# Other weight pieces get their low part by an adding transfer in the first feed-forward

## The chip, the cores and the metric

The kernel runs on one core of one Trainium2 chip. The metric is the time of one execution in device microseconds, as the median of repeated runs. TensorE (PE) does the matrix products, VectorE (DVE) and ScalarE (ACT) prepare their operands, SyncE (SP) issues the plain loads, and GpSimd (POOL) issues the transfers that add to what lies in on-chip memory.

## The reference

One encoder block for 256 tokens of width 2048 in float32. It has two feed-forwards, and between them a mixer and a cross-attention. The change touches the first feed-forward alone:

```python
def swiglu(h, w_up, w_down):
    gate, up = jnp.split(h @ w_up, 2, axis=-1)
    return (jax.nn.silu(gate) * up) @ w_down

x = x + 0.5 * swiglu(rms_norm(x, ffn1_norm[l]), ffn1_w_up[l], ffn1_w_down[l])
```

`w_up` has 2048 rows and 2 x 5632 columns, `w_down` 5632 rows and 2048 columns.

## The kernel before

**Groups and pieces.** The 5632 hidden columns are worked through in 11 groups of 512. A group needs 2048 rows of `w_up`, which come in eight pieces of 1 MB, the pairs 0 to 7: 256 rows each, that is two row blocks by the gate and the up columns of the group. After the pieces of a group come pieces of `w_down` for the groups before it: two behind groups 1 and 2, four behind group 3 and each later one. A piece is identified on the list of the plan as `("fast", g, p)`, `("mixed", g, p)` or `("down", ...)`.

**High and low parts.** A float32 product is made of three products of a rounded high part and the low part that is left: high by high, high by low and low by high. In the program's names `h` is the high part of a weight piece, `l` its low part, `xh` and `xl` those of the activations. So a row `acc<-h,xh` is a product with the weight's high part, and `acc<-l,xh` one with its low part. `three` (L587 to L600) issues the products: the first loop (L597) those with the high part, the second (L599) those with the low part.

**Seven or eight products.** A fast piece computes its 2 x 2 block product with seven block products (each as three products: 21), and needs for that differences of the weight's blocks: VectorE makes them in `td` (L321, L323, L325), and ScalarE and VectorE split `td` into the high part `h` (two halves, L146) and the low part `tl` (two halves, L147). A mixed piece does eight block products (24 products) with the weight as it is, with no `td`. Both add into the same seven PSUM banks of the group.

**Two ways to the low part.** In a piece without an adding transfer VectorE subtracts: `l = raw - h` (L147). In a piece with one, ScalarE writes the negative rounded weight into `l` (L330 for fast pieces, L276 for mixed ones), and POOL issues a transfer that adds the weight from memory once more (L331, L277), which leaves the low part. The low products of such a fast piece stand behind those with `tl`; for pair 6 they are held back into the next piece (`three(products, 3 if adds(...) else 0, ...)`). For a mixed piece with an adding transfer, load, negation and transfer begin one piece earlier (`begin_added`, L270).

**What sets the order.** The letters of `FIRST` (L46) list a group's pieces in their order: `f` fast, `a` fast with an adding transfer, `m` mixed, `M` mixed with an adding transfer, each followed by its pair. `first` (L50) turns them into the plan; `adds` (L77) asks for the letter `a`. `weights` (L240) prepares two pieces ahead. A scheduling layer then fixes the order of the instructions on each engine, which run strictly in that order. Buffers bound how far the preparation runs ahead: three of `h` (also used for the high part of `td`), three of `l`, three of `wide` (for `td`, `tl` and the evacuation), and four for loads (three `raw`, one `raw1`). A buffer is free again when TensorE, ScalarE or VectorE has read it for the last time.

```python
PIECES = "f1 a3 f0 a4 f2 a5 a6 f7"
...
KINDS = {"m": "mixed", "M": "mixed", "f": "fast", "a": "fast"}
...
def adds(name, e):
...
    return e[0] == "fast" and (name == "ffn1" or e[1] > 3) and f"a{e[2]}" in FIRST[e[1]]
```

The second feed-forward takes its own lists for groups 0 to 3, and `FIRST` for the later ones. The end of a group evacuates its seven banks (L679 to L691), forms the activation (L629, L630), turns it with TensorE (L637) and splits it into `hidop` (L641, L642). L707 adds a finished quarter to the residual `x`.

## Time and profile before

| | |
|---|---|
| median of 3 runs | 2431.85 us (2431.12 to 2434.92) |
| the profiled execution's own time | 2430.69 us |
| its span | 2428.9 us |
| TensorE busy | 2404.3 us, 99% |
| VectorE busy | 2025.2 us, 83% |
| ScalarE busy | 1542.3 us, 63% |
| mean granted clock of TensorE | 0.996 |

The profile lists the busy time of each engine, groups of instructions with the idle time ahead of them and what ended it, a chain of work that ended last, and tables by stretches of time. Products are pipelined: a product lasts about 0.39 us in the records, though the next one starts after some 0.23 us, so a busy TensorE need not be working at its best pace. A row of the list in order of time gives start, duration, engine, line and operands, and in brackets the idle time ahead and what ended it. In a row of the chain the numbers are start and duration.

### The profile page before, as it was taken

The numbers are of one execution on the slowest core, as the hardware profiler recorded it, in microseconds if no ns is written. First come the engines' busy times: TensorE is split into PE (matmuls) and PEld (weight loads), VectorE is DVE, ScalarE is ACT, GpSimd is POOL, SyncE is SP. The second block draws the span as 40 slices with busy tenths as digits, with TensorE's granted clock in tenths as the row PEclk, the third lists the DMA queues.
The fourth block names the chain that finished last, engine by engine and source line by source line (L and its number), as shares of the span: only waits on it lengthen the run. The fifth ranks groups of instructions, "written<-read, shape, count | busy, mean of one in ns | idle before, by whom it ended". The sixth has DMA issues, their size and how long they took to land.

```text
span 2428.9 us, 30888 instructions
## 1 busy us (share of the span) xinstructions
PE 2404.3 (99%) x12068; PEld 1997.9 (82%) x12068; DVE 2025.2 (83%) x2273; ACT 1542.3 (63%) x1564; POOL 118.7 (5%) x172
## 2 busy tenths in 40 slices
PE   9999999999999999999999999999999999999998
PEld 7887777888888888888888888888888888888887
DVE  7768898999999866768678666675799999999995
ACT  7756666777777664444476434555676677777774
POOL 0000000000000000000000000100000000000000
PEclk9999999999999999999999999999999999999999
DMA  8877778999999857666768766875588889999993
GB/s 306 309 249 238 243 214 252 276 276 276 276 276 277 280 193 275 243 258 232 262 244 290 294 245 244 301 266 190 200 323 312 308 273 280 273 275 268 273 278 136
DMA packets 98450, 636.62 MB, mean 262 GB/s; under 512 B 10944, under 2 KB 11456, under 8 KB 33536
## 3 DMA queue, kind: packets, MB, share of 16 engines
q1 hardware_dynamic: 74160, 493.61, 54.8%
q0 software_dynamic: 24000, 140.78, 23.7%
q8 instruction: 94, 1.54, 0.2%
q14 instruction: 52, 0.43, 0.1%
q10 hardware_dynamic: 144, 0.26, 0.0%
HBM read 597.77 MB, written 36.83 MB: 261 GB/s over the span
## 4 chain that ended last, share of the span: by engine, by line
PE 93%; DVE 2%; DMA 2%; issue 2%; ACT 1%; SPq 0%; POOL 0%; ACTq 0%; POOLq 0%; DVEq 0%
PE acc L597 33%; PE acc L599 17%; PE acc L354 11%; PE acc L379 8%; PE acc L380 8%; PE acc L385 8%; PE acc L357 6%; DMA l<-wu 2%; PE acc L637 1%; PE acc L526 1%; DVE tl L147 1%; DVE l L147 1%; ACT h L146 1%; DVE td L321 0%; PE acc L987 0%
## 5 line engine op out<-in xcount | busy, mean ns | idle before, releaser
L146 ACT ACTIVATE h<-raw 128x2048 fp32r<-128x2048 f32 (+3 forms) x422 | 691.4, 1652 | 451.2 <-PE acc L380 198.2
L147 DVE TENSOR_TENSOR l<-raw,h 128x2048 fp32r<-128x2048 f32 (+2 forms) x367 | 760.4, 2073 | 243.7 <-ACT h L146 241.1
L597 PE MATMUL acc<-h,xh 128*128 128x512 f32 x1222 | 478.1, 394 | 0.5 <-ACT h L146 0.3
L597 PE MATMUL acc<-h,xl 128*128 128x512 f32 x1222 | 475.4, 392 | 0.0
L146 ACT ACTIVATE h<-td 128x1024 fp32r<-128x1024 f32 x277 | 290.3, 1055 | 167.0 <-PE acc L597 69.9
L147 DVE TENSOR_TENSOR tl<-td,h 128x1024 fp32r<-128x1024 f32 x277 | 335.9, 1218 | 21.6 <-ACT h L146 19.9
L597 PE MATMUL acc<-h,hidop 128*128 128x512 f32 x1408 | 352.0, 391 | 0.0
L597 PEld LDWEIGHTS acc<-h,hidop 128*128 128x128 f32 x1408 | 262.6, 188 | 54.2 <-ACT h L146 0.5
L597 PEld LDWEIGHTS acc<-h,xh 128*128 128x128 f32 x1222 | 230.9, 189 | 57.3 <-ACT h L146 8.6
L379 PE MATMUL acc<-h,ops 128*128 128x512 f32 x704 | 276.3, 392 | 0.0
L380 PE MATMUL acc<-h,ops 128*128 128x512 f32 x704 | 274.2, 389 | 0.0
L597 PEld LDWEIGHTS acc<-h,xl 128*128 128x128 f32 x1222 | 230.9, 189 | 47.0
L354 PE MATMUL acc<-ops,h 128*128 128x512 f32 x896 | 217.1, 393 | 0.0
L599 PE MATMUL acc<-tl,xh 128*128 128x512 f32 x664 | 195.9, 395 | 0.2 <-DVE tl L147 0.2
L354 PEld LDWEIGHTS acc<-ops,h 128*128 128x128 f32 x896 | 164.2, 188 | 32.6
L599 PE MATMUL acc<-l,hidop 128*128 128x512 f32 x704 | 190.5, 389 | 0.0
L321 DVE TENSOR_TENSOR td<-raw 128x1024 f32<-128x1024 f32 x141 | 171.5, 1216 | 6.5 <-PE acc L599 6.3
L385 PE MATMUL acc<-l,ops 128*128 128x512 f32 x704 | 173.9, 389 | 0.0
L599 PE MATMUL acc<-l,xh 128*128 128x512 f32 x558 | 158.5, 394 | 14.0 <-DMA l<-wu 13.1
L599 PEld LDWEIGHTS acc<-l,hidop 128*128 128x128 f32 x704 | 132.1, 188 | 27.7
L385 PEld LDWEIGHTS acc<-l,ops 128*128 128x128 f32 x704 | 132.1, 188 | 27.4
L379 PEld LDWEIGHTS acc<-h,ops 128*128 128x128 f32 x704 | 132.2, 188 | 27.0
(253 smaller groups left out, 2832.3 us busy)
## 6 DMA issues: line engine op xcount, KB each, us to landing
raw<-wu SPq DMA_DIRECT2D x151, 1024.0 KB, 6.8
raw<-wd SPq DMA_DIRECT2D x88, 1024.0 KB, 7.3
l<-wu POOLq DMA_DIRECT2D x64, 768.0 KB, 7.8
raw<-win SPq DMA_DIRECT2D x40, 1024.0 KB, 4.8
raw<-wg SPq DMA_DIRECT2D x32, 1024.0 KB, 5.4
prep<-wu POOLq DMA_DIRECT2D x25, 1024.0 KB, 6.3
t<-prep POOLq DMA_DIRECT2D x25, 1024.0 KB, 4.5
raw<-t SPq DMA_DIRECT2D x25, 1024.0 KB, 6.6
```

The source lines that it names most:

```text
L146: done["high"] = act.activation(h, raw, ACT.Copy).ins
L147: done["low"] = dve.tensor_tensor(out=l, in0=raw, in1=h.bitcast(F32), op=ALU.subtract).ins
L321: dve.tensor_tensor(out=two[0], in0=raw[:, None, :512].broadcast_to([P, 2, 512]), in1=two[1], op=ALU.subtract)
L354: pe.matmul(acc, h[:, k * P:(k + 1) * P], xs[k], start=k == 0, stop=False)
L357: done["product"] = pe.matmul(acc[:, :T], l[:, k * P:(k + 1) * P], xs[k][:, :T], start=False, stop=k == KT - 1).ins
L379: pe.matmul(accs[t], x[:, t * P:][:, :P], h[j], start=first and j == 0, stop=False)
L380: pe.matmul(accs[t], x[:, T + t * P:][:, :P], h[j], start=False, stop=False)
L385: done["product"] = pe.matmul(accs[t], x[:, t * P:][:, :P], l[j], start=False, stop=last and j == 3).ins
L526: pe.transpose(acc[:, z * T + t * P:][:, :P], tile[:, t * 512 + (2 * y + z) * P:][:, :P], ident)
L597: pe.matmul(acc, a, b, start=start, stop=False)
L599: pe.matmul(acc, ah, bl, start=False, stop=stop)
L637: pe.transpose(acc[:, z * T + t * P:][:, :P], hid[t][:, (2 * y + z) * P:][:, :P], ident)
```

## The change

In groups 1 and 2 the letters change from `f1 a3 M0 f4 f2 M6 a5 f7` to `f1 f3 M0 a4 f2 M6 f5 a7`: pairs 4 and 7 get the adding transfer, and the low parts of pairs 3 and 5 are made by VectorE. Group 3 had `f1 a3 f0 a4 f2 a5 a6 f7` and gets `f1 f3 M0 a4 f2 a5 a6 f7`: pair 0 goes by eight products with an adding transfer for its low part, and the low part of pair 3 is made by VectorE. Groups 0 and 4 to 10 keep their lists, and so does the second feed-forward, which reads `FIRST` from group 4 on only.

```diff
-FIRST = ["m0 f1 m2 f3 f5 m4 f7 m6"] + ["f1 a3 M0 f4 f2 M6 a5 f7"] * 2 + [PIECES] * (NG - 3)
+FIRST = ["m0 f1 m2 f3 f5 m4 f7 m6"] + ["f1 f3 M0 a4 f2 M6 f5 a7"] * 2 + ["f1 f3 M0 a4 f2 a5 a6 f7"] + [PIECES] * (NG - 4)
```

**TensorE in group 1, pair 3.** In the kernel before, `h_2085` and `tl_2086` belong to the differences of pair 3, `l_2081` is its low part from the adding transfer, and `h_2135` is pair 0.

```order
L597 MATMUL acc_2095<-h_2085,xl_860 128x512
L599 MATMUL acc_2094<-tl_2086,xh_859 128x512
L599 MATMUL acc_2095<-tl_2086,xh_859 128x512
L599 MATMUL acc_2091<-l_2081,xh_859 128x512
L599 MATMUL acc_2092<-l_2081,xh_859 128x512
L599 MATMUL acc_2093<-l_2081,xh_859 128x512
L597 MATMUL acc_2092<-h_2135,xh_648 128x512
```

In the changed kernel `l_2081` is the low part that VectorE makes, `h_2084` and `tl_2085` belong to the differences of pair 3, and `h_2134` is pair 0.

```order
L599 MATMUL acc_2090<-l_2081,xh_859 128x512
L599 MATMUL acc_2091<-l_2081,xh_859 128x512
L599 MATMUL acc_2092<-l_2081,xh_859 128x512
L597 MATMUL acc_2093<-h_2084,xh_859 128x512
L597 MATMUL acc_2093<-h_2084,xl_860 128x512
L597 MATMUL acc_2094<-h_2084,xh_859 128x512
```

The low products of pair 3 have moved ahead of those with its differences, and they wait for VectorE and no longer for a transfer.

**ScalarE at the start of group 2, before.** `l_2460` and `h_2525` are pair 0, `l_2471`, `h_2470` and `h_2475` pair 3, `h_2425` is pair 1, and `l_2589` is the negation of pair 6.

```order
L276 ACTIVATE l_2460<-raw_2459 128x2048
L330 ACTIVATE l_2471<-raw1_2464 128x1536
L146 ACTIVATE h_2425<-td_2417 128x1024
L332 ACTIVATE h_2470<-raw1_2464 128x1536
L641 ACTIVATE hidop_2514<-acc_2509 128x2x256
L146 ACTIVATE h_2475<-td_2466 128x1024
L285 ACTIVATE h_2525<-raw_2459 128x2048
L641 ACTIVATE hidop_2522<-acc_2517 128x2x256
L146 ACTIVATE h_2475<-td_2466 128x1024
L146 ACTIVATE h_2554<-raw_2548 128x1536
L146 ACTIVATE h_2558<-td_2550 128x1024
L276 ACTIVATE l_2589<-raw_2588 128x2048
```

The same stretch of the changed kernel, where `l_2554` is the negation of pair 4, `h_2474` the differences of pair 3, `h_2524` pair 0 and `l_2589` again the negation of pair 6:

```order
L276 ACTIVATE l_2460<-raw_2459 128x2048
L146 ACTIVATE h_2470<-raw1_2464 128x1536
L146 ACTIVATE h_2425<-td_2417 128x1024
L330 ACTIVATE l_2554<-raw_2547 128x1536
L641 ACTIVATE hidop_2513<-acc_2508 128x2x256
L276 ACTIVATE l_2589<-raw_2588 128x2048
L146 ACTIVATE h_2474<-td_2466 128x1024 x2
L641 ACTIVATE hidop_2521<-acc_2516 128x2x256
L285 ACTIVATE h_2524<-raw_2459 128x2048
```

The negation of pair 6 has moved from behind pair 4 to ahead of both halves of pair 3's differences; it needs the load `raw_2588` and a free buffer of `l`.

**ScalarE at the start of group 3, before.** `l_2856`, `h_2855` and `h_2860` are pair 3, `h_2916` and `h_2920` pair 0, `h_2953` and `l_2954` pair 4, `h_2815` is pair 1.

```order
L330 ACTIVATE l_2856<-raw_2849 128x1536
L332 ACTIVATE h_2855<-raw_2849 128x1536
L146 ACTIVATE h_2815<-td_2807 128x1024
L641 ACTIVATE hidop_2899<-acc_2894 128x2x256
L146 ACTIVATE h_2860<-td_2851 128x1024
L146 ACTIVATE h_2916<-raw_2910 128x1536
L146 ACTIVATE h_2860<-td_2851 128x1024
L641 ACTIVATE hidop_2907<-acc_2902 128x2x256
L146 ACTIVATE h_2920<-td_2912 128x1024
L332 ACTIVATE h_2953<-raw_2947 128x1536
L330 ACTIVATE l_2954<-raw_2947 128x1536
```

In the changed kernel `l_2850` and `h_2914` are pair 0, `h_2860` and `h_2864` pair 3, and `l_2944` and `h_2943` pair 4.

```order
L276 ACTIVATE l_2850<-raw_2849 128x2048
L146 ACTIVATE h_2860<-raw_2854 128x1536
L146 ACTIVATE h_2815<-td_2807 128x1024
L330 ACTIVATE l_2944<-raw_2937 128x1536
L641 ACTIVATE hidop_2903<-acc_2898 128x2x256
L146 ACTIVATE h_2864<-td_2856 128x1024
L285 ACTIVATE h_2914<-raw_2849 128x2048
L641 ACTIVATE hidop_2911<-acc_2906 128x2x256
L146 ACTIVATE h_2864<-td_2856 128x1024
L332 ACTIVATE h_2943<-raw_2937 128x1536
```

The negation of pair 4, which feeds its adding transfer, has moved from behind pair 0 to ahead of the second half of group 2's hidden operand.

From group 5 on ScalarE, the plain loads and the adding transfers stand as before, and on VectorE and TensorE some neighbours are exchanged in each group. Counted over the whole program, TensorE has three products more, VectorE five instructions fewer and ScalarE two fewer.

## The prediction

> **What bounds the kernel now.** I read the page first, then who waits for whom, then tables by stretches of time, and last the rows in order of time around the waits.

> ```profile
> PE 2404.3 (99%) x12068; PEld 1997.9 (82%) x12068; DVE 2025.2 (83%) x2273; ACT 1542.3 (63%) x1564; POOL 118.7 (5%) x172
> PE 93%; DVE 2%; DMA 2%; issue 2%; ACT 1%; SPq 0%; POOL 0%; ACTq 0%; POOLq 0%; DVEq 0%
> L599 PE MATMUL acc<-l,xh 128*128 128x512 f32 x558 | 158.5, 394 | 14.0 <-DMA l<-wu 13.1
> ```

> TensorE fills the span and holds 93% of the chain, so only two things shorten the kernel: fewer products, or TensorE waiting less. The one line with a large wait is the low products of fast pieces, 13.1 us, and what they wait for is the adding transfer. All of it lies in groups 1 to 3 of the first feed-forward (the windows are cut at each group's first product; columns are length, then busy time of TensorE, weight loads, VectorE, ScalarE and GpSimd, then granted clock, share of the transfer engines, GB/s):

> ```profile
> 224.81:282.24 57.43, 54.02 (x232) 43.19 (x230) 49.24 (x53) 38.15 (x33) 3.46 (x4) 0.97 0.81 243
> 282.24:340.88 58.64, 53.09 (x231) 43.49 (x230) 48.88 (x52) 37.58 (x32) 3.44 (x4) 0.94 0.80 242
> 340.88:412.98 72.10, 66.38 (x282) 52.37 (x280) 64.58 (x69) 47.17 (x42) 4.37 (x5) 0.95 0.80 234
> 412.98:474.10 61.12, 60.93 (x271) 49.54 (x270) 60.07 (x63) 45.15 (x39) 4.35 (x5) 1.00 0.92 277
> ...
> 320.64 3.17 PE acc L597 x14
> ```

> Fourteen products in 3.17 us make 0.2264 us for one. Group 4 has eight fast pieces and four down pieces, 8 x 21 + 4 x 24 = 264 products, or 59.77 us; its 61.12 us leave 1.35 us for the turning of the hidden operand and small gaps, so it is full. By that measure group 3, with the same work, loses 72.10 - 61.12 = 11.0 us. Groups 1 and 2 have 6 x 21 + 2 x 24 + 2 x 24 = 222 products, 50.26 + 1.35 = 51.6 us, and lose 5.8 and 7.0 us. Together 23.8 us are lost in these three groups, more than the waits named. The rest is the clock:

> ```profile
> 237.01 0.73 PE L599 MATMUL acc<-l,xh 128*128 128x512 f32 x2 [2.67 <-DMA l<-wu]
> ...
> 295.92 0.79 PE L599 MATMUL acc<-l,xh 128*128 128x512 f32 x1 [5.55 <-DMA l<-wu]
> ...
> 364.95 0.79 PE L599 MATMUL acc<-l,xh 128*128 128x512 f32 x1 [4.56 <-DMA l<-wu]
> ...
> 237.90:241.20 3.30, 3.30 (x9) 2.62 (x8) 2.00 (x2) 0.00 (x0) 0.00 (x0) 0.51 0.97 405
> 295.92:299.30 3.38, 3.38 (x8) 2.70 (x9) 0.72 (x2) 0.00 (x0) 0.00 (x0) 0.52 1.01 424
> 365.00:371.00 6.00, 6.00 (x15) 4.70 (x16) 2.33 (x3) 0.00 (x0) 0.00 (x0) 0.51 1.03 291
> ```

> The three long waits stand before pair 3 of groups 1 and 2 and pair 4 of group 3. Behind each TensorE runs at half clock, for 3.3, 3.4 and 6.0 us, which costs half of that again: 1.65, 1.7 and 3.0 us. Waits and clock make 2.67 + 5.55 + 4.56 + 6.35 = 19.1 of the 23.8 us.

> Why the transfers come late is a matter of when ScalarE could write the negation and how long the transfer took (start and duration):

> ```profile
> 228.07 1.48 ACT L330 ACTIVATE l<-raw 128x1536 fp32r<-128x1536 f32 x1
> ...
> 282.44 1.49 ACT L330 ACTIVATE l<-raw 128x1536 fp32r<-128x1536 f32 x1 [2.81 <-PE acc L599]
> ...
> 353.32 1.46 ACT L330 ACTIVATE l<-raw 128x1536 fp32r<-128x1536 f32 x1
> ...
> 229.98 6.99 DMA l<-wu
> 253.32 12.41 DMA l<-wu
> 284.33 11.55 DMA l<-wu
> 355.18 9.72 DMA l<-wu
> ```

> For pair 3 the negation had to wait for a buffer or stood behind the evacuation of the group before, and TensorE was at most a piece and a half away. In group 3 pair 4's stood behind all of pair 0.

> **The change part by part.** *Work.* Durations by form, from the stretch 205 to 480 us (busy, mean ns):

> ```profile
> L147 DVE TENSOR_TENSOR tl<-td,h 128x1024 fp32r<-128x1024 f32 x63 | 76.3, 1217 | 12.2 <-ACT h L146 12.1
> L321 DVE TENSOR_TENSOR td<-raw 128x1024 f32<-128x1024 f32 x32 | 38.9, 1216 | 6.3 <-PE acc L599 6.3
> L147 DVE TENSOR_TENSOR l<-raw,h 128x1536 fp32r<-128x1536 f32 x18 | 31.5, 1751 | 4.3 <-ACT h L146 4.3
> L323 DVE TENSOR_TENSOR td<-raw,td 128x512 f32<-128x512 f32 x31 | 21.2, 683 | 0.2
> L146 ACT ACTIVATE h<-td 128x1024 fp32r<-128x1024 f32 x63 | 66.0, 1056 | 46.0 <-PE acc L597 25.2 <-DVE td L325 12.4 <-DVE tl L147 2.1
> L276 ACT ACTIVATE l<-raw 128x2048 fp32r<-128x2048 f32 x6 | 11.4, 1906 | 0.0
> ```

> Pair 0 of group 3 by eight products costs TensorE 3 x 0.2264 = 0.68 us, all on the path, and takes its differences, their split and its low part off VectorE: 1.22 + 0.68 + 0.68 (L325 is L323's form) + 2 x 1.22 + 1.75 = 6.8 us; pair 3's low part puts 1.75 us back. VectorE thus does 5.0 us less, worth nothing by itself, as it was idle 7.5 us in group 3. In groups 1 and 2 the work is the same and only stands elsewhere. ScalarE gives and takes about as much; its count falls by two.

> *Group 1.* The wait for pair 3's transfer goes. What is late next is VectorE and ScalarE:

> ```profile
> 229.54 1.22 DVE L321 TENSOR_TENSOR td<-raw 128x1024 f32<-128x1024 f32 x1
> ...
> 230.50 0.60 ACT L641 ACTIVATE hidop<-acc 128x512 fp32r<-128x512 f32 x1 [0.96 <-PE acc L637]
> ```

> Behind that VectorE row comes the low part, so it ends at 229.54 + 1.2 + 1.75 = 232.4 us, while TensorE asks at 231.5: 0.9 us. Behind that ScalarE row comes pair 4's negation (1.5 us), then half of pair 3's differences, ready at 233.5, and pair 0's high part at 235.3: two waits of some 0.4 us, and a like one at pair 2's second half. All small, no long gap: 2.0 us remain of 5.8. Pair 4's transfer starts near 232.5 and is wanted near 246.6 us; by the longest row, 12.41 us, it is in time. Pair 7's negation waits for pair 2's buffer, its transfer starts near 253.9 and is wanted at 266.7 us, the last products of the group: by 12.41 us just in time, by 9.7 well so.

> *Group 2.* It starts 3.8 us earlier. Pair 3's wait of 5.55 us goes with its clock, but ScalarE now meets pair 6's negation ahead of pair 3's halves, and stands there until pair 6's load has landed. Rows of this place, and of loads alone, with one adding transfer and with two beside them:

> ```profile
> 282.48 0.68 DVE L325 TENSOR_TENSOR td<-raw,td 128x512 f32<-128x512 f32 x1
> 283.22 0.33 SPq L275 DMA_DIRECT2D raw<-wu  x1
> ...
> raw<-wu SPq DMA_DIRECT2D x1, 1024.0 KB, 4.7
> raw<-wu SPq DMA_DIRECT2D x1, 1024.0 KB, 8.5
> raw<-wu SPq DMA_DIRECT2D x1, 1024.0 KB, 9.7
> ```

> The load goes out when pair 1's last difference (L325) frees its buffer, 3.8 to 4.3 us earlier than 283.22, at 279.0. One transfer is half done then and the next starts four us later, so I take 7.5 us, between 4.7 and 8.5 and nearer the second: landed at 286.5, negated (1.9) at 288.4, first half (1.06) at 289.4. TensorE, starting the group at 278.4 with pair 1's 21 products, nine of pair 3 and 1.35 us of turning, is there at 286.5 and waits 2.9 us. Queued behind on ScalarE are both halves, the second `hidop` and pair 0's high part, and TensorE waits for each. As 2.67 us brought the half clock, I charge it here too, but 0.65 of the 1.65 us run while pair 0's high part is awaited anyway: 1.0 us. Pair 2's load follows pair 0's high part, some 8 us to land, and its chain through VectorE comes 1.5 us late in two waits. With 0.1 for the rest, 5.5 of 7.0 us remain. Bounds: a load in 4.7 us makes no wait (2 us remain), one in 9.7 makes 5.1 us and the full clock (8.4 remain).

> [...]

> *Group 3.* Pair 4's negation moves ahead of the second `hidop`, some 15 us before its products want the transfer, and the 4.56 us go with their 3.0 us of clock. Pair 0's transfer begins two pieces early. VectorE works without a break and is the nearest thing: three or four waits of 0.2 to 0.75 us (the second turning waits for the bank that its `hidop` frees; second halves of `tl`), 1.8 us in all, of 11.0. Bounds: nothing, or one wait as pair 4's for pair 5 or 6, whose transfers start 8 to 13 us ahead of their use: 4.56 + 3.0.

> *Later.* No row from group 4 on waits for the moment at which it starts, so the shift stays to the end.

> *Sum.* 23.8 - (2.0 + 5.5 + 1.8) - 0.68 = 13.8 us gained. The profiled execution took 2430.69 us, 1.16 below the median of 2431.85; less 13.8 it is 2416.9, and the median **2418.0 us**. About 0.2%, 4.9 us, is what a measurement of this kernel can tell from no change.

> **The rivals.**

> *All waits go (5%).* Pair 6's load lands early and VectorE keeps up: 23.8 - 0.7 - 2 = 21 us gained, 2410.8. For it: the idle time of VectorE in groups 1 and 2. Against: its rows stand in a strict order, and in group 1 it is late already by the first low part.

> *The waits move to other transfers (21%).* Pair 6's load takes 9.7 us or more beside two transfers (2.9 us worse), and pair 7's transfer, or that of pair 5 or 6 in group 3, comes late once as long as pair 3's did in group 1 (2.67 + 1.65 = 4.3 us): 13.8 - 7.2 = 6.6 us gained, 2425.2. For it: transfers of 11.55 and 12.41 us, and engines at 0.97 to 1.03 when the loads bunch. Against: pair 7's neighbours, the down loads, leave earlier than now, since pair 6 and pair 2 are read earlier.

> *Nothing gained (8%).* As before, but in each group: 2.9 + 3 x 4.3 = 15.8 us lost eat the 13.8, 2433.8. That needs a late transfer in all three groups.

> *Slower: VectorE becomes the bound from group 4 on (4%).* It is busy 60.07 of 61.12 us there. TensorE arrives without the waits in which VectorE got ahead, some neighbours on VectorE are exchanged, and each idle moment beyond the 1.05 us to spare lengthens the group. From 1.05 + 13.8 / 7 = 3.0 us of idle a group it eats the gain in the seven groups 4 to 10; at 4.0 us, 2.95 x 7 = 20.7 us lost against 13.8 gained, 2438.7. Against: group 4 ran full with the same list, and VectorE has 5.0 us less to do before it.

> That the change does nothing it says is excluded: the counts on TensorE and VectorE differ by what was worked out, and the second feed-forward keeps its lists.

> **How the numbers follow.** The forecast with its bounds (10 to 18 us gained) has 62%. Range: 13.8 - 7.2 = 6.6 us at one end, 21 us at the other, **2411 to 2425.3 us**, which leaves out the 12% of no gain and slower and some edges of the rest. Faster by over 0.2%: 62 + 5 + 21 = 88%; within 0.2%: 8%; slower by over 0.2%: 4%.

> **What would show it.** Right: groups 1, 2 and 3 at about 53.6, 57.1 and 63.6 us; no wait over 1 us on a transfer there; the one long wait of TensorE, near 289 us, ended by ScalarE's `h` of pair 3, with half clock behind; group 4 again at 61.1 us. Wrong: a wait on `DMA l<-wu` of several us at a group's last products or at pair 5 or 6; group 2 as long as before; groups 4 to 10 longer than 61.1 us; or TensorE waiting for `tl` or `l` from VectorE more than 2 us a group.

## The result and the profile after

The changed kernel takes 2418.47 us (median of 3, 2417.98 to 2419.87), the one before 2431.85 (2431.12 to 2434.92): a ratio of 0.9943, 95% interval 0.992 to 0.9966. The profiled execution took 2417.98 us against 2430.69: 12.7 us less. The forecast was 2418.0 us, with 13.8 us less in the profiled execution. (A ratio here is to the kernel before, run beside the other.)

The page of the kernel after: busy times, the chain by engine, and the group of low products that carried the 13.1 us of waiting before.

```profile
PE 2399.5 (99%) x12071; PEld 1996.2 (83%) x12071; DVE 2021.0 (84%) x2268; ACT 1541.2 (64%) x1562; POOL 118.7 (5%) x172
PE 95%; DVE 2%; DMA 1%; issue 1%; ACT 1%; SPq 0%; ACTq 0%; POOLq 0%; DVEq 0%
L599 PE MATMUL acc<-l,xh 128*128 128x512 f32 x561 | 156.2, 390 | 1.2 <-DVE l L147 0.9
```

TensorE holds 95% of the chain instead of 93, with three products more, and the waits of that group for transfers have shrunk from 13.1 us to 0.3. Where the time came from stands in the windows of groups 1 to 4, and one of 3 us in group 2 (columns as before the change):

```profile
224.50:277.72 53.22, 52.17 (x231) 42.20 (x230) 48.89 (x53) 38.90 (x34) 3.46 (x4) 1.00 0.83 262
277.72:336.18 58.46, 53.70 (x231) 43.24 (x230) 49.01 (x52) 37.48 (x32) 3.44 (x4) 0.97 0.81 243
336.18:400.45 64.27, 63.44 (x284) 51.45 (x283) 62.15 (x66) 46.00 (x40) 4.37 (x5) 1.00 0.94 286
400.45:461.60 61.15, 61.15 (x273) 49.97 (x272) 59.12 (x61) 45.27 (x39) 4.35 (x5) 1.00 0.87 266
289.24:292.20 2.96, 2.96 (x7) 2.39 (x8) 2.96 (x4) 2.96 (x3) 0.26 (x1) 0.52 1.08 361
```

Group 1 is 4.2 us shorter and group 3 7.8, both now at a clock of 1.00. Group 2 is 0.2 us shorter, at 0.97, and holds the one stretch at half clock that is left. Group 4 is as it was; it starts 12.5 us earlier, and nearly all of the 12.7 us was thus gained ahead of it. The waits of TensorE in this part (us in total, times, longest):

```profile
PE acc L597 <- ACT h L146: 3.6, 2, 3.0
PE acc L599 <- DVE l L147: 0.9, 1, 0.9
PE acc L637 <- DVE hidop L642: 0.8, 2, 0.4
PE acc L599 <- DVE tl L147: 0.7, 1, 0.7
PE acc L599 <- DMA l<-wu: 0.3, 1, 0.3
```

and those of group 2, in order of time:

```profile
285.58 0.66 PE L637 MATMUL acc<-vt,ev 128*128 128x128 f32 x4 [0.41 <-DVE hidop L642]
289.24 0.80 PE L597 MATMUL acc<-h,xh 128*128 128x512 f32 x1 [3.00 <-ACT h L146]
...
292.50 1.09 PE L599 MATMUL acc<-tl,xh 128*128 128x512 f32 x4
...
306.71 0.50 PE L597 MATMUL acc<-h,xh 128*128 128x512 f32 x1 [0.65 <-ACT h L146]
...
309.75 0.73 PE L599 MATMUL acc<-tl,xh 128*128 128x512 f32 x2 [0.70 <-DVE tl L147]
```

The 5.55 us for pair 3's transfer have become 3.00 us for the high part of pair 3's differences, and the eight products with that part, from 289.24 to 292.50, take 3.26 us. ScalarE's rows, VectorE's row that makes the first half of pair 3's differences, and two rows of the chain (start and duration) say what that part waited for:

```profile
286.33 1.91 ACT L276 ACTIVATE l<-raw 128x2048 fp32r<-128x2048 f32 x1 [3.06 <-PE acc L637]
288.14 1.99 ACT L146 ACTIVATE h<-td 128x1024 fp32r<-128x1024 f32 x2
```

```profile
283.70 1.22 DVE L321 TENSOR_TENSOR td<-raw 128x1024 f32<-128x1024 f32 x1
```

```profile
278.71 7.51 DMA raw<-wu
...
292.44 8.81 DMA raw<-wu
```

ScalarE stood for 3.06 us before pair 6's negation. The row names the turning on TensorE, but the first one had ended at 282.63, and in the run with ten products (below) the second started at 288.29, behind the negation; what came last was pair 6's load, issued at 278.71 and landed at 286.22. Only then came the negation, and behind it both halves of pair 3, though the input of the first had been there since VectorE finished it at 284.92. The second load is pair 2's, which goes out when pair 0's high part has read its buffer; the waits of 0.65 and 0.70 us hang on that.

### The profile page after: what moved, and what is told of

The parts are those of the page before. It is cut to its first block, busy times and chain, and to the rows that moved or that the text cites. A ratio compares the mean times of both kernels' runs of the same rounds, so it can differ in the third digit from the quotient of the medians.

```text
span 2416.2 us, 30880 instructions
## 1 busy us (share of the span) xinstructions
PE 2399.5 (99%) x12071; PEld 1996.2 (83%) x12071; DVE 2021.0 (84%) x2268; ACT 1541.2 (64%) x1562; POOL 118.7 (5%) x172
## 4 chain that ended last, share of the span: by engine, by line
PE 95%; DVE 2%; DMA 1%; issue 1%; ACT 1%; SPq 0%; ACTq 0%; POOLq 0%; DVEq 0%
PE acc L597 34%; PE acc L599 17%; PE acc L354 11%; PE acc L379 8%; PE acc L380 8%; PE acc L385 8%; PE acc L357 6%; PE acc L637 1%; DMA raw<-wu 1%; PE acc L526 1%; DVE l L147 1%; DVE tl L147 0%; DMA l<-wu 0%; ACT h L146 0%; DVE td L321 0%
## 5 line engine op out<-in xcount | busy, mean ns | idle before, releaser
L146 ACT ACTIVATE h<-raw 128x2048 fp32r<-128x2048 f32 (+3 forms) x422 | 691.4, 1652 | 457.5 <-PE acc L380 197.8
L147 DVE TENSOR_TENSOR l<-raw,h 128x2048 fp32r<-128x2048 f32 (+2 forms) x367 | 760.9, 2074 | 240.3 <-ACT h L146 237.6
L597 PE MATMUL acc<-h,xh 128*128 128x512 f32 x1221 | 476.1, 392 | 3.9 <-ACT h L146 3.6
L597 PE MATMUL acc<-h,xl 128*128 128x512 f32 x1221 | 473.8, 391 | 0.0
L146 ACT ACTIVATE h<-td 128x1024 fp32r<-128x1024 f32 x275 | 288.0, 1055 | 151.1 <-PE acc L597 55.8
L597 PE MATMUL acc<-h,hidop 128*128 128x512 f32 x1408 | 351.5, 391 | 0.0
L147 DVE TENSOR_TENSOR tl<-td,h 128x1024 fp32r<-128x1024 f32 x275 | 333.8, 1220 | 20.1 <-ACT h L146 18.4
L597 PEld LDWEIGHTS acc<-h,hidop 128*128 128x128 f32 x1408 | 262.7, 188 | 53.9
L597 PEld LDWEIGHTS acc<-h,xh 128*128 128x128 f32 x1221 | 229.7, 188 | 58.7 <-ACT h L146 9.2
L597 PEld LDWEIGHTS acc<-h,xl 128*128 128x128 f32 x1221 | 229.8, 188 | 46.7
L599 PE MATMUL acc<-tl,xh 128*128 128x512 f32 x660 | 193.1, 394 | 0.8 <-DVE tl L147 0.7
L599 PE MATMUL acc<-l,hidop 128*128 128x512 f32 x704 | 190.7, 389 | 0.0
L321 DVE TENSOR_TENSOR td<-raw 128x1024 f32<-128x1024 f32 x140 | 170.5, 1218 | 4.5 <-DMA raw<-wu 4.2
L599 PE MATMUL acc<-l,xh 128*128 128x512 f32 x561 | 156.2, 390 | 1.2 <-DVE l L147 0.9
L599 PEld LDWEIGHTS acc<-l,hidop 128*128 128x128 f32 x704 | 132.2, 188 | 27.6
## 6 DMA issues: line engine op xcount, KB each, us to landing
raw<-wu SPq DMA_DIRECT2D x151, 1024.0 KB, 6.8
raw<-wd SPq DMA_DIRECT2D x88, 1024.0 KB, 7.3
raw<-win SPq DMA_DIRECT2D x40, 1024.0 KB, 4.9
raw<-wg SPq DMA_DIRECT2D x32, 1024.0 KB, 5.0
prep<-wu POOLq DMA_DIRECT2D x25, 1024.0 KB, 6.8
t<-prep POOLq DMA_DIRECT2D x25, 1024.0 KB, 4.5
raw<-t SPq DMA_DIRECT2D x25, 1024.0 KB, 6.5
```

The source lines that it names most:

```text
L146: done["high"] = act.activation(h, raw, ACT.Copy).ins
L147: done["low"] = dve.tensor_tensor(out=l, in0=raw, in1=h.bitcast(F32), op=ALU.subtract).ins
L321: dve.tensor_tensor(out=two[0], in0=raw[:, None, :512].broadcast_to([P, 2, 512]), in1=two[1], op=ALU.subtract)
L597: pe.matmul(acc, a, b, start=start, stop=False)
L599: pe.matmul(acc, ah, bl, start=False, stop=stop)
```

## The experiments

The theory: in each group the gain is the one long wait that the group's own list removes, and the half clock behind it; the groups add up; in group 2 a new wait on ScalarE, behind pair 6's load, took nearly all of it back. The rivals: the gain comes from VectorE's lighter load in group 3, the waits only move on, or the half clock has nothing to do with idle time. Group lengths in us, each cut at the groups' first products:

| | group 1 | group 2 | group 3 | median of the runs |
|---|---|---|---|---|
| before | 57.43 | 58.64 | 72.10 | 2431.85 |
| after | 53.22 | 58.46 | 64.27 | 2418.47 |
| groups 1 and 2 alone | 53.22 | 58.16 | 72.06 | 2426.81 |
| group 3 alone | 57.66 | 60.13 | 64.63 | 2423.70 |
| group 2 undone | 53.23 | 59.11 | 64.66 | 2420.31 |
| pair 6 of group 2 by VectorE | 53.28 | 52.52 | 64.62 | 2411.90 |
| ten products in the wait | 53.30 | 57.50 | 64.39 | 2418.19 |
| pair 6 of group 2 later | 53.22 | 52.63 | 65.15 | 2412.95 |
| group 3, pair 0 as before | 53.23 | 58.76 | 70.91 | 2425.58 |
| group 3, pair 3 as before | 53.22 | 59.95 | 71.15 | 2423.84 |
| pair 6 of group 1 by VectorE too | 54.62 | 52.00 | 64.48 | 2413.01 |
| four products in the wait | 53.24 | 58.30 | 64.34 | 2418.16 |

The kernel before, run beside them, had medians of 2430.93 us (for the first four experiments of the table), 2430.69 (the next four) and 2431.83 (the last two). Each group length is from one profiled execution.

**Groups 1 and 2 alone.** Group 3 gets its list of before back (these diffs show the lists alone).

```diff
-["f1 f3 M0 a4 f2 a5 a6 f7"]
+["f1 a3 f0 a4 f2 a5 a6 f7"]
```

> Groups 1 and 2 have the new lists, group 3 the one of the kernel before. Theory (a group's gain is the one long wait and the half clock that its own list removes; groups simply add up): groups 1 and 2 take 53.2 and 58.5 us as in the changed kernel, group 3 the 72.1 us of before; gain 4.2 + 0.2 + 0.3 ahead of group 1 = 4.7 us, 2427.2 us. Rival A (the gain comes from VectorE's 6.8 us less work on pair 0 of group 3): no gain here, 2431.9 us. Rival B (a group that starts earlier meets its loads later, so the waits move on): group 3 takes up to 4.4 us longer than 72.1 us, and the time stays at 2431 us although groups 1 and 2 got shorter.

Measured: 2426.81 us, ratio 0.9983 (0.9974 to 0.9992). Group 3 in this run, to the length of before:

```profile
336.20:408.26 72.06, 65.98 (x282) 52.12 (x280) 64.60 (x69) 47.16 (x42) 4.37 (x5) 0.95 0.77 234
```

Group 3 starts 4.7 us earlier and is as long as before, with a wait of 4.87 us on a transfer. So the shift is kept (against rival B) and the gain of group 1 needs nothing of group 3 (against rival A).

**Group 3 alone.** Groups 1 and 2 get `f1 a3 M0 f4 f2 M6 a5 f7` back.

```diff
-["f1 f3 M0 a4 f2 M6 f5 a7"] * 2
+["f1 a3 M0 f4 f2 M6 a5 f7"] * 2
```

> Only group 3 has its new list, groups 1 and 2 those of the kernel before. Theory: groups 57.4, 58.6 and 64.3 us, the waits on the adding transfers of pair 3 (2.7 and 5.6 us) still there, that of pair 4 in group 3 gone; gain 7.8 us, 2424.0 us. Rival A (VectorE's work in group 3 is the whole gain): the gain is all of 13.4 us, 2418.5 us. Rival B (waits move on): group 3 keeps a wait of several us on another transfer, because the pieces ahead of it differ, and takes 68 us or more, 2428 us.

Measured: 2423.70 us, ratio 0.9969 (0.9957 to 0.9981), 7.2 us under the kernel before beside it. Group 3 takes 64.63 us at the full clock; groups 1 and 2 keep their waits:

```profile
236.19 1.35 PE L599 MATMUL acc<-l,xh 128*128 128x512 f32 x3 [2.78 <-DMA l<-wu]
...
295.41 0.80 PE L599 MATMUL acc<-l,xh 128*128 128x512 f32 x1 [5.76 <-DMA l<-wu]
```

The two parts gained 4.1 and 7.2 us, together 11.3 of the 13.4 between the medians; group 2, with its list of before, was 1.5 us longer here (60.13 us) than in the kernel before. Its wait ended at 295.41 us, and the products behind it ran at half clock to 301.42, 6.0 us and not the 3.3 of before (the last section has both in steps), which makes 1.4 of the 1.5 us:

```profile
294.59:298.00 3.41, 2.59 (x6) 2.12 (x7) 1.34 (x2) 0.00 (x0) 0.00 (x0) 0.50 1.02 430
298.00:301.42 3.42, 3.42 (x9) 2.66 (x9) 0.00 (x0) 0.00 (x0) 0.00 (x0) 0.50 0.80 335
```

The theory holds for groups 1 and 3.

**Group 2 undone.** Only group 2 goes back to its list of before.

```diff
-["f1 f3 M0 a4 f2 M6 f5 a7"] * 2
+["f1 f3 M0 a4 f2 M6 f5 a7", "f1 a3 M0 f4 f2 M6 a5 f7"]
```

> Groups 1 and 3 have the new lists, group 2 the one of the kernel before. Theory: group 2's new list only exchanged one wait (5.55 us on pair 3's transfer) for another (3.0 us on ScalarE behind pair 6's negation, and small ones), so its undoing costs nothing: group 2 58.3 to 59 us, groups 1 and 3 53.2 and 64.3 us, 2418.7 us, the same as the changed kernel within 0.5 us. Rival (group 2's list is worth the 1.5 us that the prediction gave it, or group 3 rests on it): 2420 us or more, with group 2 at 60 us or group 3 at 66 us.

Measured: 2420.31 us (2418.58 to 2420.71), ratio 0.9952 (0.9937 to 0.9967). The group lengths are close to the theory's, but the median is 1.8 us above the changed kernel's and not within 0.5 us of it, where the rival put it. The two ratios' intervals overlap, so the medians don't decide.

```profile
277.63:336.74 59.11, 53.86 (x231) 44.07 (x230) 48.91 (x52) 38.02 (x32) 3.44 (x4) 0.94 0.81 241
```

```profile
291.01 0.80 PE L599 MATMUL acc<-l,xh 128*128 128x512 f32 x1 [5.25 <-DMA l<-wu]
```

The old wait is back, and group 2 is 0.65 us longer than in the changed kernel, group 3 0.4. With either list group 2 differed from run to run by more than that (58.16 to 59.95 us with the new one, 58.64 to 60.13 with the old), so what the new one is worth in group 2 lies between nothing and some 2 us; this run does not say it closer. It is a fraction of what the removed wait had cost.

**Pair 6 of group 2 by VectorE.** The letter `M` becomes `m` in group 2: eight products still, the low part from VectorE, no negation on ScalarE and no transfer.

```diff
-["f1 f3 M0 a4 f2 M6 f5 a7"] * 2
+["f1 f3 M0 a4 f2 M6 f5 a7", "f1 f3 M0 a4 f2 m6 f5 a7"]
```

> The changed kernel with pair 6 of group 2 by eight products without an adding transfer: VectorE makes its low part (one instruction of 128x2048, some 2.3 us), and ScalarE has no negation of pair 6 to do ahead of pair 3's halves. Theory (the head-of-line wait on ScalarE is what ate group 2's gain): the 3.0 us wait near 289 us goes, and the half clock behind it (1.4 us), and what came late after it (1.0 to 1.5 us): group 2 takes 53 to 54.5 us, 2413 to 2415 us. Rival A (VectorE, 49 us busy in that group and now 51.3, becomes its bound): group 2 56 to 58 us with waits of TensorE for l and tl of VectorE, 2416 to 2418 us. Rival B (the wait of 3.0 us stood for pair 3's own load and not for the negation): group 2 stays at 58.5 us, 2418.5 us.

Measured: 2411.90 us (2411.72 to 2412.32), ratio 0.9918 (0.9902 to 0.9935). The window of group 2, ScalarE's first half of pair 3, and TensorE at the same place:

```profile
277.57:330.09 52.52, 52.06 (x232) 42.26 (x230) 50.57 (x53) 36.15 (x31) 2.57 (x3) 1.00 0.80 250
```

```profile
284.86 1.06 ACT L146 ACTIVATE h<-td 128x1024 fp32r<-128x1024 f32 x1 [1.75 <-DVE td L321]
```

```profile
285.97 0.50 PE L597 MATMUL acc<-h,xh 128*128 128x512 f32 x1
```

The half is written 3.3 us earlier, TensorE goes straight on where it waited 3.00 us, the clock stays full, and group 2 is 5.9 us shorter. Group and median came out a little below the theory's ranges. VectorE, at 50.57 of 52.52 us, does not hold it up (rival A), and pair 3's own load was there in time (rival B). This is the lowest median of all, though the intervals of the ratios do not tell it from the version with pair 6 later, nor from the one with pair 6 of group 1 by VectorE too.

**Pair 6 of group 2 later.** The adding transfer stays, but pairs 5 and 6 change places.

```diff
-["f1 f3 M0 a4 f2 M6 f5 a7"] * 2
+["f1 f3 M0 a4 f2 M6 f5 a7", "f1 f3 M0 a4 f2 f5 M6 a7"]
```

> The changed kernel with pairs 6 and 5 of group 2 exchanged: pair 6 keeps its eight products and its adding transfer, but its load, negation and transfer begin one piece later, behind pair 2 on ScalarE and no longer ahead of pair 3's halves. VectorE's work is that of the changed kernel. Theory (only the place of the negation in ScalarE's order cost the 3.0 us and what followed): group 2 takes 52.5 to 54 us as with the low part by VectorE, 2412 to 2413.5 us. Rival (pair 6's transfer, begun one piece later and with pair 7's right behind it, comes late now): a wait on a transfer of 2 to 4 us and half clock in the last third of group 2, 55 to 58 us, 2415 to 2418 us.

Measured: 2412.95 us (2412.78 to 2413.22), ratio 0.9926 (0.9911 to 0.994).

```profile
277.13:329.76 52.63, 52.17 (x231) 42.16 (x230) 47.42 (x52) 37.69 (x32) 3.44 (x4) 1.00 0.85 267
```

Group 2 is as short as without the transfer, with VectorE at 47.42 us; group 3 is 0.9 us longer than in the changed kernel (65.15 us), with 1.1 us more of VectorE's work in it. It was thus not that pair 6 has a transfer, nor VectorE's load, but the place of one instruction that waits, ahead of instructions that could have run. The load and the transfer moved with the negation here; that it was the negation that held up the rest is what ScalarE's rows of the changed kernel show.

**Ten products in the wait.** Useless products on TensorE, ahead of the second turning in group 2; their bank is written anew, so the outputs don't change.

```diff
                 acc = bank()
+                if name == "ffn1" and g == 1 and y == 1:
+                    for _ in range(10):
+                        pe.matmul(acc, pairs[0][0][0][:, :P], hids[0][:, :512], start=True, stop=True)
```

> The changed kernel with ten useless products (128x512 each, into a bank that the turning of the hidden operand writes anew behind them) on TensorE, right where it waits 3.0 us for pair 3's first half in group 2. They take 10 x 0.2264 = 2.26 us of that wait and delay nothing, and leave some 1 us idle. Theory (the half clock behind the wait comes from TensorE's being idle): the products behind the wait keep the full clock, 0.23 us apart and not 0.43, and group 2 gets 1.4 us shorter, 57.1 us for 58.5; 2417 us. Rival (the half clock comes from what else goes on there, the load and the adding transfer on the move at once, and not from the idle time): the products stay 0.43 us apart and group 2 at 58.5 us.

Measured: 2418.19 us, ratio 0.9948 (0.9934 to 0.9963).

```profile
285.89 2.56 PE L637 MATMUL acc<-hidop,xh 128*128 128x512 f32 x10 [0.41 <-DVE hidop L645]
...
289.29 0.50 PE L597 MATMUL acc<-h,xh 128*128 128x512 f32 x1 [0.39 <-ACT h L146]
...
291.27 1.15 PE L599 MATMUL acc<-tl,xh 128*128 128x512 f32 x4
...
303.26 0.50 PE L597 MATMUL acc<-h,xh 128*128 128x512 f32 x1 [0.65 <-ACT h L146]
...
307.07 0.50 PE L597 MATMUL acc<-h,xh 128*128 128x512 f32 x1 [1.25 <-ACT h L146]
```

```profile
289.29:292.25 2.96, 2.96 (x12) 2.20 (x13) 2.96 (x3) 2.96 (x3) 0.27 (x1) 1.00 1.02 342
```

Pair 3's half came at the same moment (289.29 against 289.24) and the transfer engines were as busy (1.02 against 1.08), yet the clock stayed at 1.00, while group 2 has its stretch of half clock in each of the other five versions with this list that keep the wait (the changed kernel, groups 1 and 2 alone, four products, and both versions with half of group 3's edit: a mean of 0.97 over group 2 in each, and 1.00 here). The half clock thus went with TensorE's idle time there, 3.00 us in the changed kernel and 0.39 here, and the rival falls. The eight high products behind the wait took 1.98 us (289.29 to 291.27) instead of 3.26. Group 2 is 0.96 us shorter, less than these 1.28 us and than the 1.4 expected, while the waits of pair 2's chain grew from 1.35 to 1.90 us. The 0.96 us are the difference of two single executions, smaller than what group 2 differed by between runs with the same list, and the median did not move measurably. ScalarE's evacuation of the turned operand also fell behind pair 0's high part here.

**Four products in the wait.** The same with `range(4)`.

```diff
-                    for _ in range(10):
+                    for _ in range(4):
```

> As the version with ten useless products ahead of the wait in group 2, but with four of them: 0.9 us of the 3.0 us are filled, 2.1 us stay idle. Theory (the half clock comes with an idle time from somewhere between 0.4 and 2.7 us on, the longest without it and the shortest with it): either the products behind the wait keep 0.23 us, and the limit lies between 2.1 and 2.7 us, or they go to 0.43 us for some 3 us, and it lies below 2.1 us. I expect the full clock, as the waits of 2.09 us in another run (pair 0 of group 3) had no half clock behind them; group 2 57.5 us. Rival: half clock, group 2 58.5 us.

Measured: 2418.16 us, ratio 0.9944 (0.9924 to 0.9964).

```profile
289.03 0.79 PE L597 MATMUL acc<-h,xh 128*128 128x512 f32 x1 [2.12 <-ACT h L146]
```

```profile
289.03:292.53 3.50, 3.50 (x8) 2.79 (x9) 3.50 (x4) 3.50 (x4) 0.27 (x1) 0.51 1.10 348
```

My expectation missed: some 3.4 us of half clock (0.51) stood behind 2.12 us of idle time, and group 2 took 58.30 us, as the rival had it. The last section sets this gap beside the one of 2.09 us in another run.

**Group 3, pair 0 as before.** Pair 3's low part by VectorE as in the changed kernel, pair 0 by seven products.

```diff
-["f1 f3 M0 a4 f2 a5 a6 f7"]
+["f1 f3 f0 a4 f2 a5 a6 f7"]
```

> Groups 1 and 2 as in the changed kernel; in group 3 pair 3's low part by VectorE as there, but pair 0 by seven products with its low part by VectorE, as before. Pair 4's negation stands ahead of the second hidden operand here too. TensorE has three products (0.68 us) less, VectorE 6.8 us more: 69 us of work for a group of 64.3. Theory (in group 3 the gain is the transfer of pair 4 that starts earlier, but it needs the 6.8 us that VectorE loses): no wait on pair 4's transfer, but VectorE is the bound and group 3 takes 69 to 70.5 us, 2423 to 2424.5 us. Rival (VectorE, idle 7.5 us in that group before, has the room): 63.6 to 65 us, 2417.5 to 2419 us.

Measured: 2425.58 us, ratio 0.9979 (0.997 to 0.9989), 1 us above the theory's range. The first 29 us of group 3, and the waits of TensorE there and behind:

```profile
337.01:366.00 28.99, 26.18 (x114) 19.93 (x112) 28.92 (x31) 20.61 (x19) 2.30 (x3) 1.00 0.66 185
```

```profile
352.82 0.50 PE L597 MATMUL acc<-h,xh 128*128 128x512 f32 x1 [2.09 <-ACT h L146]
...
369.02 1.65 PE L599 MATMUL acc<-l,xh 128*128 128x512 f32 x3 [3.07 <-DMA l<-wu]
```

VectorE works 28.92 of 28.99 us while TensorE waits. The waits are named after ScalarE and a transfer, which stand behind VectorE in turn: ScalarE waits for `td`, and pair 5's negation behind that, whose transfer then comes 3.07 us late. VectorE is the bound, and its 6.8 us were worth about as much in group 3: 70.91 - 64.27 = 6.6. But the theory's way to that length was only half right: it had no late transfer in it, and the 3.07 us on pair 5's, with the half clock behind (0.50 from 368.81 to 372.22 us), are the larger part of the 6.6.

**Group 3, pair 3 as before.** Pair 0 by eight products as in the changed kernel, pair 3 with its adding transfer.

```diff
-["f1 f3 M0 a4 f2 a5 a6 f7"]
+["f1 a3 M0 a4 f2 a5 a6 f7"]
```

> Groups 1 and 2 as in the changed kernel; in group 3 pair 0 by eight products with an adding transfer as there, but pair 3 keeps its adding transfer as before. VectorE has 1.75 us less to do than in the changed kernel, ScalarE one negation more, and three transfers (pairs 0, 3 and 4) go out near the group's start. Theory (transfers near a group's start come late for pair 3, as they did in groups 1 and 2 before): a wait on pair 3's transfer of 1 to 5 us with half clock behind it, group 3 66 to 70 us, 2420 to 2424 us. Rival (the move of pair 0 alone is the whole edit, pair 3's low part by VectorE was not needed): group 3 63.5 to 64.5 us, 2417.5 to 2418.5 us.

Measured: 2423.84 us, ratio 0.9972 (0.9961 to 0.9984). The wait, the transfer ahead of it in the chain, and the clock behind it:

```profile
352.22 1.65 PE L599 MATMUL acc<-l,xh 128*128 128x512 f32 x3 [5.16 <-DMA l<-wu]
```

```profile
340.64 11.53 DMA l<-wu
```

```profile
352.20:358.00 5.80, 5.78 (x14) 4.53 (x15) 0.00 (x0) 0.69 (x1) 0.00 (x0) 0.50 1.01 304
```

Pair 3's transfer has the fate that it had in groups 1 and 2 before, and 71.15 us are 1.2 more than the expectation's upper end. So group 3 needed both of its edits; either one alone leaves it at 71 us, near the 72.10 of before.

**Pair 6 of group 1 by VectorE too.** The version with pair 6 of group 2 by VectorE, with `M` to `m` in group 1 as well.

```diff
-["f1 f3 M0 a4 f2 M6 f5 a7", "f1 f3 M0 a4 f2 m6 f5 a7"]
+["f1 f3 M0 a4 f2 m6 f5 a7"] * 2
```

> As the version with pair 6 of group 2 by eight products and its low part by VectorE, with pair 6 of group 1 treated the same way. In group 1 ScalarE met no load that was not there, so its negation of pair 6 held nobody up. Theory (what counts is a negation that stands on ScalarE waiting for its load, and there is none in group 1): nothing to gain, group 1 53.2 us and group 2 52.5 us, 2411.9 us, the same. Rival A (every adding transfer less makes the loads faster): group 1 52.5 us, 2411.2 us. Rival B (VectorE, late at group 1's start, gets 2.3 us more to do): TensorE waits longer for l and tl, group 1 54 to 55 us, 2413 us.

Measured: 2413.01 us (2411.71 to 2413.26), ratio 0.9921 (0.9905 to 0.9938): no gain, as the theory had it. But group 1 is 1.3 us longer, and it and the median have the lengths that rival B gave. Another wait than it named makes most of that, one on a transfer at the group's last products; what made this transfer late no run shows:

```profile
267.11 0.96 PE L599 MATMUL acc<-l,xh 128*128 128x512 f32 x3 [1.10 <-DMA l<-wu]
```

## Why the prediction was right, and where it was not

- **What bounds the kernel: right.** Three waits on transfers and the clock behind them. Groups 1 and 3 lost them and gained 4.2 and 7.8 us (forecast 3.8 and 8.5); each part alone gave its share. That the median came within 0.5 us is partly luck: the profiled execution gained 12.7 us and not 13.8, group 1 gave more and groups 2 and 3 less than forecast, and the median was taken to lie 1.16 us above the profiled execution, where it lay 0.49 above.
- **Group 1: right.** 53.22 us (53.6). The wait of 0.9 us for VectorE's low part came at 0.86; the three small ones of some 0.4 us did not come at that size.
- **Group 2: the mechanism was right, the size was not.** The wait behind pair 6's negation was there at 289.24 us with 3.00 us (forecast 2.9), from a load of 7.51 us (7.5; the forecast chose that between rows of 4.7 and 8.5, so to hit it so closely was luck). But group 2 took 58.46 us, not 57.1. Against the full group of 51.6 us it loses 6.9 us, not 5.5: 3.00 for that wait, 1.45 for the clock (eight products in 3.26 us, at 0.2264 each 1.81), 1.35 for pair 2's chain (1.5), 0.41 for the second turning, and some 0.65 of small gaps. **The terms that were mis-sized are "1.0" for the clock and "0.1 for the rest"** (1.45 and 1.06 measured). The forecast hid 0.65 us of the half clock behind a wait for pair 0's high part. That part was ready at 292.42 us, and at full clock TensorE would have asked for it near 292.2 (estimate, from 289.24 and the pace of the run with ten products), so only some 0.2 us could hide there. What the half clock cost group 2 in the end stays open: the run with ten products has 0.96 us, near the forecast's 1.0, but as a difference of two single executions. The turning's 0.41 us I had counted in group 3 and forgotten here.
- **Group 3: right, 0.7 us too short.** 64.27 us (63.6). Waits of 0.41 and 0.35 us and a `tl` that came 0.2 us late make 1.0 of the 2.5 us that it takes beyond group 4 and its three more products. Some 0.8 us more were never to be won: "with the same work" as group 4 was wrong, as group 3 turns two hidden operands, that of group 2 and its own (16 products at L637, before and after, against 8 in group 4). The row below has the second, 0.79 us until the next product at 394.92. VectorE as the nearest thing held: given its 6.8 us back, it set the length, the larger part by way of a late transfer.

```profile
394.13 1.03 PE L637 MATMUL acc<-vt,ev 128*128 128x128 f32 x8
```

- **The rivals.** VectorE as the bound from group 4 on did not come: group 4 takes 61.15 us. Waits on other transfers did not come in the changed kernel (0.3 us in all), but they did in other versions: 1.10 us at pair 7 of group 1 without pair 6's transfers, and in group 3, with half of its edit, 3.07 us at pair 5 or 5.16 us at pair 3.
- **What the forecast missed to ask** is that the wait it saw coming could be avoided: with the letter `m` for pair 6 of group 2, or with that pair one place later, the kernel takes 2411.9 or 2413.0 us.

## What to carry to other kernels

An engine that runs its instructions strictly in order should not be given one that waits for a load ahead of others whose inputs are there: one negation placed so cost group 2 nearly 6 us here, and with it one piece later the kernel was 5.5 us shorter. Price a gap on TensorE by its own length plus the slower products behind it (3.00 and 1.45 us in group 2 of the changed kernel), and ask of the latter what they would have waited for anyway. When two edits stand in one group, try each alone: here both single edits of group 3 were worth about 1 us, and the two together 7.8.

## What the runs showed of the hardware

```profile
285.61:289.02 3.41, 1.30 (x8) 0.87 (x6) 0.92 (x3) 2.90 (x3) 0.59 (x1) 1.00 0.98 193
289.02:292.43 3.41, 3.40 (x8) 2.73 (x9) 3.41 (x4) 3.41 (x4) 0.28 (x1) 0.50 1.13 357
```

The gap of 2.09 us (group 3, pair 0 as before; it ends at 352.82 us) is split between two steps, each over 2 us busy, and the step behind them is at full clock:

```profile
348.33:351.74 3.41, 2.39 (x10) 1.30 (x8) 3.38 (x5) 1.19 (x3) 0.86 (x1) 1.00 1.06 308
351.74:355.15 3.41, 2.14 (x8) 1.50 (x9) 3.38 (x4) 3.36 (x3) 0.00 (x0) 1.00 0.90 177
355.15:358.57 3.42, 3.42 (x17) 2.83 (x16) 3.42 (x5) 2.56 (x2) 0.00 (x0) 1.00 0.86 329
```

In the kernel before and in the changed one, every such step at full clock in which TensorE was idle 1.99 us or more by the records was followed by one at half clock, and none with 1.13 us or less was. The step with the 1.99 us, from group 2 of the kernel before, and one with 1.53 us from group 3 alone, which was not followed by half clock:

```profile
288.95:292.36 3.41, 1.42 (x9) 0.89 (x7) 3.41 (x5) 3.41 (x5) 0.00 (x0) 1.00 1.06 245
287.76:291.18 3.42, 1.89 (x11) 1.24 (x9) 3.42 (x5) 3.42 (x4) 0.00 (x0) 1.00 1.10 273
```

With groups 1 and 2 alone a wait of 2.81 us ended at 289.36, the products ran at full clock for 1.2 us more, and the half clock came with the next step and not with the first product behind the gap:

```profile
287.11:290.52 3.41, 1.16 (x5) 0.88 (x6) 1.24 (x3) 3.41 (x4) 0.86 (x1) 1.00 1.01 250
290.52:293.94 3.42, 3.42 (x10) 2.64 (x9) 3.39 (x5) 3.42 (x4) 0.00 (x0) 0.50 0.99 297
```

In group 3 of the kernel before and in group 2 of group 3 alone (the first of the two rows shown with that run), a step at half clock that itself held 0.92 and 0.82 us of idle time was followed by another one; steps at half clock with 0.45 us or less were followed by full clock, in the kernel before and in the changed one. The wait of 5.55 us in group 2 of the kernel before had 3.3 us of products at half clock behind it, the one of 5.76 us at the same place with group 3 alone 6.0 us. What sets these steps no run tests.

**Loads beside adding transfers.** In the changed kernel pair 6's load of 1 MB took 7.51 us with two adding transfers on the move, and pair 2's 8.81 us with one and with other loads, where one by itself had taken 4.7 in the kernel before. The busy share of the transfer engines was 1.03 and 0.98 during these two; what made them longer no run tests.
